# The norm of four mixers: squares summed into columns instead of rows, and the factor turned back into rows by a matmul

## Chip, cores, metric

The kernel runs on one core of a Trainium2 chip. The metric is the time of one execution in microseconds (us). The engines are TensorE (PE, with its weight loads PEld), VectorE (DVE), ScalarE (ACT), GpSimd (POOL) and the DMA queues of SyncE (SP). A program that is compiled from the kernel fixes the order of the instructions on each engine.

## What is computed

A network of two blocks over 256 tokens of width 1024, all in float32. The first block (attention, gated delta rule, mixture of experts) is not touched. The second has four layers, each a mixer and an MLP, each between norms:

```python
def rms_norm_2(x, gain):
    xf = x.astype(jnp.float32)
    y = xf * lax.rsqrt(jnp.mean(xf * xf, axis=-1, keepdims=True) + RMS_EPS) * gain.astype(jnp.float32)
    return y.astype(x.dtype)

def second_block(x, norm_gains, ...):
    h = x
    for i in range(DEPTH_2):                      # 4
        kind, j = i % N_MIXERS, i // N_MIXERS     # 3 kinds
        xn = rms_norm_2(h, norm_gains[i, 0])
        if kind == 0:
            m = stick_breaking_mixer(xn, sb_w_qkv[j], sb_w_o[j])
        elif kind == 1:
            m = short_conv_mixer(xn, conv_w_in[j], conv_w[j], conv_w_out[j])
        else:
            m = gla_mixer(xn, gla_w_in[j], ...)
        h = h + rms_norm_2(m, norm_gains[i, 1])
        f = squared_relu_mlp(rms_norm_2(h, norm_gains[i, 2]), ffn_w_up[i], ffn_w_down[i])
        h = h + rms_norm_2(f, norm_gains[i, 3])
    return h
```

The change concerns `rms_norm_2(h, norm_gains[i, 0])`, the norm ahead of each mixer. So the mixers come in the order stick-breaking, conv, GLA, stick-breaking.

## The kernel before

The residual is kept transposed: `hT` is 128 partitions x 8 chunks x 256 tokens, so the width lies across partitions and chunks and the tokens lie along the free axis. A norm therefore has to sum squares over partitions, which PE does.

Stages follow each other through `post` (L426). It turns the result of the stage before into `hT`, chunk by chunk (transposes L444, addition on DVE L447), and at once makes the operand of the next stage: `operand` splits gain x `hT` in two parts of reduced precision, `xh` (ACT, L348) and `xl` (DVE, L349). The matmuls of the mixer begin on these *un-normalised* operands. What is missing is one factor per token. It is applied when products leave PSUM: `ev_q` and `ev_k` (L723, L728) in the stick-breaking mixer, L582 in the conv mixer, L810 and L824 in GLA.

The factor `r` has the row form: 128 x 256, every partition the same. `pre` returns a function `factor()` that makes it when it is first asked for. For a mixer it does so in two steps, with a priority of 50 ahead of its place in the program:
- `sumsq(..., direct=8)`: eight squares on ACT (L324) and eight f32 matmuls `ones` x square, 128 x 256, into one PSUM bank of tag `s` (L337). With `ones` as the weights every partition gets the sums.
- `factor`: Ln (L290) and Exp (L291) on ACT, then four DVE instructions L294 to L297 for a corrected inverse root, all 128 x 256.

Where the mixer's values are evicted with tokens on the partitions, the factor is needed as a column per token. `columns` (L696) makes it from `r` with two transposes (L700) and a DVE copy. The two stick-breaking mixers and GLA do that.

Weights come by DMA as `raw` pieces of 128 x 1024, and `split` parts each into a cast `hi` (ACT, L190) and a rest `lo` (DVE, L193). The names `mg` and `split` are two further pairs of buffers for the same. `chunk` (L220) makes 128 columns of a product with 24 matmuls of 128 x 256: eight times `hi` x `xh` (L228) and `lo` x `xh` (L229), then eight of `hi` x `xl` (L231). `chunks` alternates the PSUM tags `g` and `s`; each tag has two banks. So a product that is not evicted holds its bank, and the third chunk of a tag waits for it.

The order on each engine is set by a scheduler at build time: it goes by priority, and `high_priority(offset)` moves a piece of the program ahead. Each engine then runs its instructions strictly in that order. The splits of the first weight pieces and the norm's root share DVE and ACT.

## Time and profile before

| | us |
|---|---|
| median of 3 runs | 1893.52 |
| lowest, highest | 1893.19, 1896.58 |
| profiled execution | 1894.69 |
| its span | 1892.9 |

The span is the time between the first and last recorded instruction; 1.8 us lie around it. PE is busy for 96% of it, DVE for 58%, ACT for 50%. The mean clock granted to PE is 0.988 of full speed. A row of a timeline has the start in us from the span's beginning, the duration, the engine, the line, the operation, its tiles as out<-in, the shape, and the number of records; in brackets stands how long the engine had been idle, and what ended that. A matmul of the sums leaves two records, so a pair of one-column sums is an x4. Consecutive matmuls overlap in the records, so the step from one start to the next tells what one costs.

### The profile page before, as it was taken

To read this page: it belongs to the slowest core of one execution; us is meant where nothing else is said; L and a number is where in the kernel's file an instruction comes from. 1 tells how busy PE (TensorE), PEld (TensorE's weight loads), DVE (VectorE), ACT (ScalarE), POOL (GpSimd) and SP (SyncE) were. 2 spreads that over 40 slices of the span, in tenths; PEclk is the share of its full clock that TensorE was granted. 3 is DMA by queue.
4 is the path that set the end of the run, shared out by engine and by line. 5 is a ranking of instruction groups with operands and counts; after the bars stand their busy time and mean duration, and the time that the engine had idled before them with its cause. 6 is when DMAs were issued, how large, how long until landed. Compare 5 with 4: busy or idle time off the path is not lost.

```text
span 1892.9 us, 31009 instructions
## 1 busy us (share of the span) xinstructions
PE 1825.3 (96%) x12535; PEld 1572.1 (83%) x12535; DVE 1097.2 (58%) x1964; ACT 951.5 (50%) x1743; POOL 105.2 (6%) x116
## 2 busy tenths in 40 slices
PE   6899998998999999999999999999999999999998
PEld 3787788866666798899999899979989988989996
DVE  4848547532332664765577665567775556547554
ACT  4536456322222575644454654465664447746443
POOL 2212112100000000000011000001000000000000
PEclk9899999999999999999999999999999999999999
DMA  9544386688999443555545555543446554345561
GB/s 328 178 164 144 96 275 255 217 309 329 408 396 392 132 148 124 167 183 195 180 154 185 171 180 198 182 143 113 134 156 196 183 191 131 131 138 184 176 197 45
DMA packets 196872, 369.46 MB, mean 195 GB/s; under 512 B 9204, under 2 KB 153012, under 8 KB 185204
## 3 DMA queue, kind: packets, MB, share of 16 engines
q1 hardware_dynamic: 193248, 362.77, 55.8%
q10 hardware_dynamic: 2900, 3.29, 0.5%
q8 instruction: 100, 1.64, 0.3%
q0 software_dynamic: 576, 1.37, 0.3%
q14 instruction: 48, 0.39, 0.1%
HBM read 364.77 MB, written 2.63 MB: 194 GB/s over the span
## 4 chain that ended last, share of the span: by engine, by line
PE 70%; ACT 4%; DVE 2%; issue 1%; POOL 0%; DVEq 0%; ACTq 0%; POOLq 0%
PE big L530 22%; PE g L228 8%; PE g L229 8%; PE g L231 7%; PE g L1808 4%; PE s L1848 3%; PE s L231 2%; PE s L228 2%; PE s L229 2%; PE s L337 1%; ACT sq L415 1%; ACT sbs L750 1%; ACT sbs L749 1%; PE big L1860 1%; PE s L1777 1%
## 5 line engine op out<-in xcount | busy, mean ns | idle before, releaser
L193 DVE TENSOR_TENSOR lo<-raw,hi 128x1024 fp32r<-128x1024 f32 x310 | 382.1, 1235 | 268.2 <-ACT hi L190 260.7
L190 ACT CAST hi<-raw 128x1024 fp32r<-128x1024 f32 x318 | 331.4, 1045 | 213.0 <-PE big L530 121.6
L228 PE MATMUL g<-xh,hi 128*128 128x256 f32 x1088 | 277.4, 290 | 8.8 <-DVE glal L810 3.6
L229 PE MATMUL g<-xh,lo 128*128 128x256 f32 x1088 | 272.9, 286 | 0.7 <-DVE lo L193 0.7
L228 PEld LDWEIGHTS g<-xh,hi 128*128 128x128 f32 x1088 | 208.5, 192 | 21.4 <-issue 6.0
L229 PEld LDWEIGHTS g<-xh,lo 128*128 128x128 f32 x1088 | 208.7, 192 | 3.4 <-DVE lo L193 0.9
L231 PE MATMUL g<-xl,hi 128*128 128x256 f32 x1088 | 155.0, 284 | 0.0
L231 PEld LDWEIGHTS g<-xl,hi 128*128 128x128 f32 x1088 | 141.0, 192 | 0.3 <-issue 0.2
L530 PE MATMUL big<-hi,yh 128*128 128x512 f32 x416 | 133.7, 392 | 0.0
L530 PE MATMUL big<-hi,yl 128*128 128x512 f32 x416 | 133.2, 390 | 0.0
L530 PE MATMUL big<-lo,yh 128*128 128x512 f32 x416 | 133.0, 390 | 0.0
L493 ACT ACTIVATE sq<-g 128x256 f32<-128x256 f32 x116 | 44.5, 384 | 166.9 <-PE g L231 166.6
L193 DVE TENSOR_TENSOR split<-raw,split 128x1024 fp32r<-128x1024 f32 x64 | 78.3, 1224 | 58.2 <-ACT split L190 58.1
L193 DVE TENSOR_TENSOR mg<-raw,mg 128x1024 fp32r<-128x1024 f32 x64 | 78.3, 1224 | 53.9 <-ACT mg L190 53.8
L190 ACT CAST split<-raw 128x1024 fp32r<-128x1024 f32 x64 | 66.9, 1045 | 62.7 <-PE big L530 40.5
L190 ACT CAST mg<-raw 128x1024 fp32r<-128x1024 f32 x64 | 66.9, 1046 | 50.2 <-PE big L530 32.6
L530 PEld LDWEIGHTS big<-lo,yh 128*128 128x128 f32 x416 | 78.1, 188 | 16.9
L530 PEld LDWEIGHTS big<-hi,yl 128*128 128x128 f32 x416 | 78.1, 188 | 16.6
L228 PE MATMUL s<-xh,hi 128*128 128x256 f32 x320 | 84.5, 296 | 3.6 <-DVE fv L294 2.5
L530 PEld LDWEIGHTS big<-hi,yh 128*128 128x128 f32 x416 | 75.4, 188 | 13.9 <-issue 0.3
L229 PE MATMUL s<-xh,lo 128*128 128x256 f32 x320 | 83.1, 292 | 2.2 <-DVE lo L193 2.2
L271 DVE TENSOR_TENSOR yl<-s,yh 128x256 fp32r<-128x256 f32 x76 | 32.1, 423 | 87.7 <-ACT yh L270 81.2
(575 smaller groups left out, 4090.6 us busy)
## 6 DMA issues: line engine op xcount, KB each, us to landing
raw<-in_ffn_w_up_dram SPq DMA_DIRECT2D x64, 1024.0 KB, 5.7
raw<-in_ffn_w_down_dram SPq DMA_DIRECT2D x64, 1024.0 KB, 4.8
raw<-in_w_mod_dram SPq DMA_DIRECT2D x24, 1024.0 KB, 6.7
raw<-in_sb_w_qkv_dram SPq DMA_DIRECT2D x24, 1024.0 KB, 5.2
raw<-in_w_in_dram SPq DMA_DIRECT2D x22, 1024.0 KB, 6.7
raw<-in_conv_w_in_dram SPq DMA_DIRECT2D x12, 1024.0 KB, 5.4
raw<-in_gla_w_in_dram SPq DMA_DIRECT2D x12, 1024.0 KB, 5.4
extra<-in_w_e_gate_dram SPq DMA_DIRECT2D x11, 1024.0 KB, 9.0
```

Source lines behind the costliest of these rows:

```text
L190: i = nc.scalar.copy(hi, piece)
L193: j = on.tensor_tensor(out=lo, in0=piece, in1=hi.bitcast(F32), op=ALU.subtract)
L228: mm(ps, hi[:, k, sl], xh[k], start=k == 0, stop=False)
L229: mm(ps, lo[:, k, sl], xh[k], start=False, stop=False)
L231: mm(ps, hi[:, k, sl], xl[k], start=False, stop=k == kn - 1)
L271: self.nc.vector.tensor_tensor(out=lo, in0=src, in1=hi.bitcast(F32), op=ALU.subtract)
L337: mm(ps, self.ones, t, start=i == 0, stop=i == len(terms) - 1)
L415: nc.scalar.activation(out=junk, in_=acc[t][half], func=AF.Square, accum_out=o)
L493: nc.scalar.activation(out=t, in_=ps, func=AF.Relu)
L530: mm(acc[t][half], x[:, t * P:(t + 1) * P], v[:, 0, half * 512:(half + 1) * 512], start=g + c + i == 0, stop=g + c == n - 1 and i == 2, sk ...
L1808: on(mm(gu[i][64 * j:64 * j + 64, :], xg[:, k, o0 + j * cap:o0 + (j + 1) * cap], W[j][k], start=k == 0, stop=k == KD - 1, skip_group_check ...
L1848: on(mm(yps[64 * j:64 * j + 64, :], aT[:, f * P + 64 * j:f * P + 64 * j + 64], W[j][f][:, half * 512:half * 512 + 512], start=f == 0, stop ...
```

## The change

The norm of the mixers is made by other instructions.
- The sums: `column_sums` takes the square as the *weights* and one column of ones as the moving operand: for each of eight chunks and each half of the tokens one f32 matmul of 128 x 1 (L412 of the changed kernel). The result is two columns with tokens on the partitions. A whole bank of tag `s` is taken for it.
- The root: `column_factor` does Ln, Exp and the four DVE instructions on 128 x 2 (L421 to L426).
- The row form: for each half of the tokens DVE multiplies `ones` by the factor column (`fq`, `fv`, L379), a matmul with the identity turns that into 128 rows of the factor (L380, in f32, into the other half of the same bank), and ACT copies both halves to `r` (L381).
- The columns are kept as `self.rcol` for the values, and `columns` with its transposes goes.
- From the root on, the priority is 2000 ahead instead of 50.

```diff
                     with self.tc.high_priority(offset=50):
-                        ps = self.sumsq([self.hT[:, k] for k in range(KD)], nc.gpsimd, direct=8)
-                        self.factor(ps, D, r)
+                        bank = self.gps("s")
+                        self.column_sums(bank[:, 0:2])
+                    with self.tc.high_priority(offset=2000):
+                        self.rcol = self.column_factor(bank[:, 0:2])
+                        for t in range(2):
+                            m = self.nt("fv", 1)[:, :P] if t else self.nt("fq", 1)[:, :P]
+                            nc.vector.tensor_scalar(out=m, in0=self.ones, scalar1=self.rcol[:, t:t + 1], scalar2=None, op0=ALU.mult)
+                            nc.tensor.matmul(bank[:, S + t * P:S + (t + 1) * P], m, self.c["ident"], start=True, stop=True)
+                        nc.scalar.copy(r, bank[:, S:])
...
+    def column_sums(self, ps):
+
+        nc, order = self.nc, []
+        for k in range(KD):
+            sq = self.nt("sq", 3)
+            nc.scalar.activation(out=sq, in_=self.hT[:, k], func=AF.Square)
+            for t in range(2):
+                order.append(nc.tensor.matmul(ps[:, t:t + 1], sq[:, t * P:(t + 1) * P], self.ones[:, 0:1], start=k + t == 0,
+                                              stop=k == KD - 1, skip_group_check=True))
+        self.after(order[1], order[0])
+
+    def column_factor(self, ps):
+
+        nc = self.nc
+        st = self.pn.tile([P, 8], F32, tag="rst", name="rst", bufs=2)
+        v, y, q, r = [st[:, i:i + 2] for i in range(0, 8, 2)]
+        nc.scalar.activation(out=y, in_=ps, func=AF.Ln, scale=1.0 / D, bias=self.eps[:, 0:1])
+        nc.scalar.activation(out=y, in_=y, func=AF.Exp, scale=-0.5)
+        nc.vector.tensor_scalar(out=v, in0=ps, scalar1=1.0 / D, scalar2=EPS, op0=ALU.mult, op1=ALU.add)
+        nc.vector.tensor_tensor(out=q, in0=y, in1=y, op=ALU.mult)
+        nc.vector.scalar_tensor_tensor(out=q, in0=q, scalar=-0.5, in1=v, op0=ALU.mult, op1=ALU.mult)
+        nc.vector.scalar_tensor_tensor(out=r, in0=q, scalar=1.5, in1=y, op0=ALU.add, op1=ALU.mult)
+        return r
...
-    def columns(self, rep, out):
-
-        ps = self.gps("s")
-        for t in range(2):
-            self.nc.tensor.transpose(ps[:, t * P:(t + 1) * P], rep[:, t * P:(t + 1) * P], self.c["ident"])
-        self.nc.vector.tensor_copy(out, ps[:, 0:S].rearrange("p (t q) -> p t q", q=P)[:, :, 0])
-
...
-        rc = self.tmp(2, tag="sbrc", bufs=1)
-        self.columns(r(), rc)
+        r()
+        rc = self.rcol
...
-        rc = self.tmp(2, tag="glrc", bufs=1)
-        self.columns(r(), rc)
+        r()
+        rc = self.rcol
```

The order of instructions changes with it. On PE in the conv mixer, the end of the sums; before, L337 is a row sum and L228, L229 and L231 are the matmuls of chunks (`hi` of tag `g` the first, of `s` the second):

```order
L229 MATMUL s<-xh,lo 128x256
L228 MATMUL s<-xh,hi 128x256
L337 MATMUL s<-sq,ones 128x256
L228 MATMUL g<-xh,hi 128x256
L229 MATMUL g<-xh,lo 128x256
L231 MATMUL g<-xl,hi 128x256 x8
```

and now, where L412 is a pair of column sums:

```order
L228 MATMUL g<-xh,mg 128x256
L228 MATMUL g<-xh,hi 128x256
L229 MATMUL g<-xh,lo 128x256
L231 MATMUL g<-xl,hi 128x256
L412 MATMUL s<-ones,sq 128x1 x2
L231 MATMUL g<-xl,hi 128x256 x2
L412 MATMUL s<-ones,sq 128x1 x2
L231 MATMUL g<-xl,hi 128x256 x5
```

The last sum has moved from ahead of the last `xh` matmuls of the first chunk to among its `xl` matmuls, and parts of the second and third chunk (`mg`) come before it: 44 matmuls of chunks stand ahead of the end of the sums. In GLA there are 33, in the first mixer 22, in the last 44.

On PE in the conv mixer, the passage from the third chunk to the fourth, whose weights are in `split`, before:

```order
L228 MATMUL g<-xh,mg 128x256
L229 MATMUL g<-xh,mg 128x256
L231 MATMUL g<-xl,mg 128x256 x8
L228 MATMUL s<-xh,split 128x256
L229 MATMUL s<-xh,split 128x256
```

and now:

```order
L229 MATMUL g<-xh,mg 128x256
L231 MATMUL g<-xl,mg 128x256 x8
L380 MATMUL s<-ident,fq 128x128
L380 MATMUL s<-ident,fv 128x128
L228 MATMUL s<-xh,split 128x256
L229 MATMUL s<-xh,split 128x256
```

The two products of the row form stand between the chunks, and the fourth chunk takes a bank of tag `s` behind them. In the first mixer they stand inside the third chunk, 37 matmuls behind the last sum and 13 ahead of the fourth chunk; in the last mixer behind the first, second and fourth chunk and four mask products (L739 before), ahead of the third.

On DVE in GLA, the splits (L193) and the root, before:

```order
L193 TENSOR_TENSOR lo<-raw,hi 128x1024
L294 TENSOR_SCALAR fv<-s 128x256
L193 TENSOR_TENSOR lo<-raw,hi 128x1024
L295 TENSOR_TENSOR fq<-fy 128x256
L193 TENSOR_TENSOR lo<-raw,hi 128x1024
L296 SCALAR_TENSOR_TENSOR fq<-fq,fv 128x256
L193 TENSOR_TENSOR mg<-raw,mg 128x1024
L297 SCALAR_TENSOR_TENSOR r<-fq,fy 128x256
L810 TENSOR_TENSOR glal<-g,r 128x256
```

and now:

```order
L193 TENSOR_TENSOR lo<-raw,hi 128x1024
L423 TENSOR_SCALAR rst<-s 128x2
L424 TENSOR_TENSOR rst<-rst 128x2
L193 TENSOR_TENSOR lo<-raw,hi 128x1024
L425 SCALAR_TENSOR_TENSOR rst<-rst 128x2
L193 TENSOR_TENSOR lo<-raw,hi 128x1024
L426 SCALAR_TENSOR_TENSOR rst<-rst 128x2
L193 TENSOR_TENSOR mg<-raw,mg 128x1024
L379 TENSOR_SCALAR fq<-ones,rst 128x128
L379 TENSOR_SCALAR fv<-ones,rst 128x128
L834 TENSOR_TENSOR glal<-g,r 128x256
```

One split fewer stands between the first and the second step of the root; three still stand between the second step and the builds. ACT has, in all four mixers, a cast, Ln, a cast, Exp, two or more casts and then the copy of `r`; before, it had the same without the copy. The order of DMA issues on SP is unchanged.

## Rows read from the trace of the kernel before

**Rows 1.** Page, busy time of an engine, and the chain that ended last by engine.
```profile
PE 1825.3 (96%) x12535; PEld 1572.1 (83%) x12535; DVE 1097.2 (58%) x1964; ACT 951.5 (50%) x1743; POOL 105.2 (6%) x116
...
PE 70%; ACT 4%; DVE 2%; issue 1%; POOL 0%; DVEq 0%; ACTq 0%; POOLq 0%
```
**Rows 2.** Windows: stretch, its length, busy PE PEld DVE ACT POOL, clock, DMA.
```profile
973.00:1040.00 67.00, 67.00 (x524) 65.35 (x523) 48.12 (x77) 28.40 (x32) 11.68 (x13) 1.00 0.57 183
...
1571.50:1588.00 16.50, 16.50 (x124) 15.46 (x122) 14.31 (x28) 11.99 (x23) 0.00 (x0) 1.00 0.39 127
```
**Rows 3.** Timeline of the conv mixer's norm: PE, ACT and DVE.
```profile
957.83 0.39 PE L228 MATMUL g<-xh,hi 128*128 128x256 f32 x1
...
964.38 0.47 ACT L290 ACTIVATE fy<-s,eps 128x256 f32<-128x256 f32 x1
...
964.75 1.04 ACT L190 CAST hi<-raw 128x1024 fp32r<-128x1024 f32 x1
...
965.69 0.41 ACT L291 ACTIVATE fy<-fy 128x256 f32<-128x256 f32 x1
...
965.98 1.21 DVE L193 TENSOR_TENSOR lo<-raw,hi 128x1024 fp32r<-128x1024 f32 x1
...
967.12 0.42 DVE L295 TENSOR_TENSOR fq<-fy 128x256 f32<-128x256 f32 x1
...
970.06 0.41 DVE L297 SCALAR_TENSOR_TENSOR r<-fq,fy 128x256 f32<-128x256 f32 x1
970.12 0.28 PE L228 MATMUL s<-xh,split 128*128 128x256 f32 x1
```
**Rows 4.** Timeline of GLA's norm, PE: its first matmul, and the wait.
```profile
1242.35 0.39 PE L228 MATMUL g<-xh,hi 128*128 128x256 f32 x1
...
1255.52 0.55 PE L228 MATMUL g<-xh,hi 128*128 128x256 f32 x1 [3.59 <-DVE glal L810]
```
**Rows 5.** Timeline of PE: a pair of one-column sums in an ffn.
```profile
829.35 0.50 PE L403 MATMUL g<-ones,ss 128*128 128x1 f32 x4
...
829.91 0.28 PE L229 MATMUL g<-xh,lo 128*128 128x256 f32 x1
830.03 0.29 PE L228 MATMUL g<-xh,hi 128*128 128x256 f32 x1
```
**Rows 6.** Timeline of PE: a row sum in GLA's norm.
```profile
1247.87 0.59 PE L337 MATMUL s<-sq,ones 128*128 128x256 f32 x2
...
1248.42 0.28 PE L229 MATMUL g<-xh,lo 128*128 128x256 f32 x1
```
**Rows 7.** Timeline of ACT and DVE: small instructions of another root.
```profile
951.65 0.20 ACT L420 ACTIVATE st<-st 128x1 f32<-128x1 f32 x1 [0.29 <-DVE st L419]
...
952.12 0.16 DVE L422 TENSOR_TENSOR st<-st 128x1 f32<-128x1 f32 x1 [0.50 <-ACT st L421]
```
**Rows 8.** Timeline of PE in the first block: two f32 products of 128 columns.
```profile
80.63 0.74 PE L1148 MATMUL big<-cst,dgm 128*128 128x128 f32 x4
81.21 0.51 PE L1149 MATMUL big<-dgg,cst 128*128 128x1 f32 x4
```
**Rows 9.** Timeline of PE in the last mixer: first chunk, mask products behind the fourth.
```profile
1571.54 0.39 PE L228 MATMUL s<-xh,hi 128*128 128x256 f32 x1
...
1586.73 0.50 PE L739 MATMUL big<-maskb,identb 128*128 128x384 bf16 x2
```
**Rows 10.** Timeline of PE in the first mixer: first chunk, fourth chunk.
```profile
643.36 0.39 PE L228 MATMUL g<-xh,hi 128*128 128x256 f32 x1 [1.53 <-ACT xh L348]
...
656.51 0.28 PE L228 MATMUL s<-xh,split 128*128 128x256 f32 x1
```
**Rows 11.** Timeline of PE in the first mixer: two transposes of r.
```profile
712.29 0.44 PE L700 MATMUL s<-ident,r 128*128 128x128 f32 x2
...
712.69 0.28 PE L691 MATMUL g<-lo,xh 128*128 128x256 f32 x1
```
**Rows 12.** Windows: a stretch behind GLA's wait.
```profile
1258.00:1261.00 3.00, 3.00 (x10) 1.97 (x10) 0.69 (x1) 2.15 (x4) 0.00 (x0) 0.50 0.02 6
```

## The prediction

> **What bounds the kernel now.** I read the page first: TensorE (PE) is busy for 96% of the span, and the chain that ended last runs through it for 70%, with 4% on ACT and 2% on DVE [rows 1]. The reader is to see that a matmul saved or added is worth its own time, and that work on DVE and ACT counts only where PE waits for it. So I looked second at the stretches in which the changed norm lies, one for each mixer of the second block. In the last mixer's PE is busy for the whole 16.50 us, and after the conv norm it stays busy for 67.00 of 67.00 us [rows 2]. There is no slack that could take a delay back. Third I read the timeline of each norm, row by row, to see which value PE gets last.
>
> In the conv norm PE begins its first chunk at 957.83, Ln starts on ACT at 964.38, the factor r is written by DVE at 970.06 + 0.41 = 970.47, and PE passes from the third chunk to the fourth at 970.12 without a pause [rows 3]. That is the point: before, no matmul needs r. It is applied when products are evicted, so PE runs on through sums, root and splits. Of the four mixers only GLA holds PE up for the factor, 3.59 us, since the gate product needs an evicted operand [rows 4].
>
> **The sums: a wash.** Removed are eight sums per mixer, `ones` x squares, 256 columns wide. Added are eight pairs with the squares as weights and one column. In the GLA norm a row sum starts at 1247.87 and one chunk matmul lies between it and the matmul that starts at 1248.42; a chunk matmul takes 0.12 (829.91 to 830.03 [rows 5]), so a row sum takes 1248.42 - 0.12 - 1247.87 = 0.43 [rows 6]. The trace has products with one column too: a pair of the ffn's token sums starts at 829.35, and after one chunk matmul the next stands at 829.91, so a pair takes 0.44 [rows 5]. It is the same operation in the same place (f32, two instructions, four records), so I take 8 x 0.44 against 8 x 0.43: +0.1 per mixer, counted at nothing. Should the row be mostly something else, the pair is worth less; a lower end of 0.1 makes a rival.
>
> The Trainium skill speaks against my price here: "TensorE: Matmul & The Clock Gate", section "Back-to-back issue gap", gives about 60 cycles for the fewest columns, which at 2.4 GHz would make four records 0.1 us, and the sums 2.8 us per mixer cheaper. The pair in the trace, 0.44, doesn't agree; the same page's section "LDWEIGHTS (loading the stationary operand)" has a load cost its columns / 1.2, some 107 ns for 128, four of which come near the row.
>
> **The root: columns in place of rows, but the same queue.** Four DVE instructions and two on ACT of 256 columns become small ones; added are two builds of ones x factor (DVE, 128x128), two f32 products with the identity (PE) and a copy of r on ACT. A small DVE instruction takes 0.16 [rows 7] against 0.41 [rows 3], a small ACT one 0.20 [rows 7] against 0.47 and 0.41 [rows 3]. A build lies between 0.16 and 0.41, I take 0.28; the copy of 256 columns I take as 0.45, by Ln's 0.47. DVE: 4 x 0.19 + 2 x 0.3 = 1.4 against at most 4 x 0.41 = 1.6: nothing. ACT: 0.2 + 0.2 + 0.45 against 0.47 + 0.41: nothing. What grows is the chain, since it is longer and PE is in it now.
>
> From the end T of the last column sum: Ln at T + 0.1 for 0.2; ACT's queue has a weight cast behind it, and casts step by 965.69 - 964.75 = 0.94 [rows 3]; then Exp 0.2, so that the first DVE product of the root can run at T + 1.5. The order in front.md shows three splits still standing between that and the build of `fq`, as before: a split and a small instruction step by 1.14 + 0.2 (965.98 to 967.12 [rows 3]). So 1.5 + 0.2 + 2 x 1.34 + 1.15 = 5.5: `fq` is built from T + 5.5. The name of the change says that the root comes ahead of the splits; in the order it doesn't. Builds end at T + 5.8 and T + 6.1, the two products at T + 6.6: two f32 products of 128 columns take 81.21 - 80.63 = 0.58 [rows 8], I count 0.55 with waits between. Copy on ACT 0.45: r at T + 7.05. PE's next chunk in a bank of tag `s` stands behind the products in PE's own order and needs the bank that the copy frees, so it starts at T + 7.1. Here PE waits twice where it waited for nothing: for the builds, and for the copy. Queued behind are all matmuls of the mixer.
>
> **T, mixer by mixer.** The order also moves the last column sums behind more chunk matmuls, since the scheduler pulls other chunks forward.
> - Conv: 44 chunk matmuls and eight pairs: T = 957.83 + 44 x 0.12 + 8 x 0.45 + 0.2 (first start) = 966.9, where the row sums were done before 964.38. Chunk four starts at 966.9 + 7.1 = 974.0 against 970.12 [rows 3]: +3.9.
> - GLA: 33 matmuls: T = 1242.35 + 4.0 + 3.6 + 0.2 = 1250.1. r at 1257.15, 0.3 later still if the clock is at half, then the gate eviction of 0.42; PE starts at 1258.0 against 1255.52 [rows 4]: +2.5.
> - Last mixer (stick-breaking): 44 matmuls: T = 1571.54 + 5.3 + 3.6 + 0.2 = 1580.6. Here the scheduler puts the fourth chunk ahead of the third, which then starts at 1587.7 and ends 24 x 0.12 = 2.9 later at 1590.6. Before, all four chunks and the first mask products were through at 1586.73 + 0.8 = 1587.5 [rows 9]: +3.1.
> - First mixer (stick-breaking): 22 matmuls: T = 643.36 + 2.6 + 3.6 + 0.2 = 649.8. Here the products stand inside the third chunk, 37 matmuls (4.4) behind T, and wait there until T + 5.85. They end at 656.4; 13 more matmuls, 1.6, and the fourth chunk starts at 658.0 against 656.51 [rows 10], the copy long done: +1.5, and up to 0.5 more if the squares come late; I take 1.7.
>
> **Removed behind that.** Three times the two transposes of r and a DVE copy. A pair starts at 712.29 and, after one chunk matmul, 712.69 follows: 0.28 [rows 11]; three of them 0.75, hidden by nothing. The DVE copy lies beside PE's work, nothing.
>
> Sum: 3.9 + 2.5 + 3.1 + 1.7 - 0.75 = **+10.45 us**. The profiled execution takes 1894.69 (span 1892.9 and 1.8 around it), 1.2 above the median of the three runs, 1893.52; the sum on the median gives **1904.0** (profiled: 1905.1). T can be off by 0.5 per mixer and the chain by 0.4, all the same way: 1900.5 to 1907.5.
>
> **Rivals.**
> - *The clock falls in the new pauses.* In GLA, PE's wait of 3.59 [rows 4] is followed by a stretch at a granted clock of 0.50, the level of 1.2 GHz [rows 12]. The records at that level run from 1255.5 to about 1261, 5.5 us at half rate: 2.75 lost. The new pauses of the conv mixer (3.3 in two pieces) and of the last mixer (2.2) are shorter than 3.59, but near it. For: the size. Against: the products fall into the pause. One fall gives 1906.8, two 1909.5.
> - *Part of the delay comes back.* If the last sums are nearer to the front than I count (pairs that overlap with the chunk beside them), or if the first mixer's products find their operands ready, two of the four delays shrink to 1 or less: +3 to +7, 1896 to 1900.5. Against: PE is busy in all of [rows 2].
> - *Columns are nearly free.* At 0.1 a pair, T comes 2.8 earlier in each mixer and PE has 2.8 less to do. Then conv +1.1 (971.2 against 970.12, PE waits for the same chain), GLA -0.3, last +0.3, first -0.8, transposes -0.75: -0.45, so 1893, no change. This is what the issue gap of the Trainium skill's "TensorE: Matmul & The Clock Gate" would bring; 0.44 in [rows 5] speaks against it.
> - *Faster.* It decides whether r is there when PE comes to the fourth chunk. If pairs are cheap and the splits between turn out to be done by then, nothing waits: 4 x (2.8 - 0.55) + 0.75 = 9.7 saved, 1884. For: fewer columns for PE. Against: the order has the splits there, each 1.21 on DVE [rows 3].
>
> **How the numbers follow.** Forecast 0.54, clock 0.20, part given back 0.13, free columns 0.08, faster 0.05. The range takes in the first three: 1896 to 1911; the likeliest alone is 1900.5 to 1907.5. A measurement of this kernel tells about 0.2% (3.8 us) from no change: under 1889.7 lies the fast case, 0.05; between there and 1897.3 lie the free columns and the low end of the part given back, 0.13; above, 0.82.
>
> **What would show it.** In the trace of the changed kernel: pairs of 0.44; the conv's Ln at about 967.0 in place of 964.4; `fq` built 5.5 after the last sum, with splits before it; waits of PE for `fq` of about 2.5 and for the copy of r of about 0.65 in the conv mixer, 1.6 and 0.65 in the last, 1.4 in the first; GLA's wait up from 3.6 to about 6; two transposes gone in three mixers. I am wrong if a pair takes much less than 0.4, if the build follows the last sum by under 4 us, or if the granted clock falls after the new pauses.

## The result, and the profile after

The changed kernel takes 1905.54 us, the median of 5 runs (1904.06 to 1911.12), beside 1893.52 for the kernel before on the same chip (5 runs, 1892.9 to 1896.58). The ratio is 1.0065 (95% interval 1.0052 to 1.0077): 12 us slower. The forecast was 1904.0, slower.

The share of busy time tells nothing of it: PE is busy for 96% of the span in both. What answers to [rows 4] is the list of PE's waits; the columns are the waiting instruction, what released it, us in total, times, and the longest:

```profile
PE s L380 <- DVE fq L379: 6.5, 3, 3.4
...
PE s L228 <- ACT r L381: 0.9, 2, 0.5
PE g L228 <- DVE glal L834: 0.9, 1, 0.9
```

All three lines are new, in this form: PE waits three times for the builds of the row form, twice for the copy of r, and in GLA for the gate eviction, where the one wait of 3.59 stood before. The conv mixer answers to [rows 3] (timeline: start, duration, engine, line, instruction, and in brackets the idle time and what ended it):

```profile
959.91 0.39 PE L228 MATMUL g<-xh,hi 128*128 128x256 f32 x1
...
967.74 0.50 PE L412 MATMUL s<-ones,sq 128*128 128x1 f32 x4
968.11 0.48 PE L231 MATMUL g<-xl,hi 128*128 128x256 f32 x2
968.43 0.50 PE L412 MATMUL s<-ones,sq 128*128 128x1 f32 x4
...
968.97 0.26 ACT L421 ACTIVATE rst<-s,eps 128x2 f32<-128x2 f32 x1 [1.94 <-PE s L412]
...
970.30 0.17 DVE L424 TENSOR_TENSOR rst<-rst 128x2 f32<-128x2 f32 x1 [0.88 <-ACT rst L422]
970.38 1.22 DVE L193 TENSOR_TENSOR lo<-raw,hi 128x1024 fp32r<-128x1024 f32 x1
...
971.58 1.22 DVE L193 TENSOR_TENSOR lo<-raw,hi 128x1024 fp32r<-128x1024 f32 x1
...
972.79 1.22 DVE L193 TENSOR_TENSOR lo<-raw,hi 128x1024 fp32r<-128x1024 f32 x1
973.93 0.28 DVE L379 TENSOR_SCALAR fq<-ones,rst 128x128 f32<-128x128 f32 x1
...
974.26 0.49 PE L380 MATMUL s<-ident,fq 128*128 128x128 f32 x2 [1.87 <-DVE fq L379]
...
975.01 0.37 ACT L381 COPY r<-s 128x256 f32<-128x256 f32 x1 [1.54 <-PE s L380]
975.43 0.58 PE L228 MATMUL s<-xh,split 128*128 128x256 f32 x1 [0.46 <-ACT r L381]
```

Read it downwards. A pair of column sums costs 968.43 - 967.74 - 2 x 0.12 = 0.45. Ln starts when the last is done; three splits of 1.22 stand between the second step of the root and the build; PE, idle, takes the products, and then waits for the copy. PE's first matmul of this mixer starts at 959.91, so the fourth chunk comes 15.52 behind it, against 970.12 - 957.83 = 12.29 before.

The same in GLA, with its first matmul, and in the last mixer:

```profile
1248.46 0.39 PE L228 MATMUL g<-xh,hi 128*128 128x256 f32 x1
...
1261.52 0.76 PE L380 MATMUL s<-ident,fq 128*128 128x128 f32 x2 [3.43 <-DVE fq L379]
...
1263.62 0.58 PE L228 MATMUL g<-xh,hi 128*128 128x256 f32 x1 [0.92 <-DVE glal L834]
```
```profile
1592.83 0.49 PE L380 MATMUL s<-ident,fq 128*128 128x128 f32 x2 [1.20 <-DVE fq L379]
...
1594.01 0.38 PE L228 MATMUL s<-xh,split 128*128 128x256 f32 x1 [0.46 <-ACT r L381]
```

In the first mixer PE has two waits that it didn't have before, of 0.44 each, one among the sums and one behind them for a cast, and none for the builds:

```profile
643.33 0.39 PE L228 MATMUL g<-xh,hi 128*128 128x256 f32 x1 [0.44 <-ACT xh L348]
...
656.88 0.39 PE L380 MATMUL s<-ident,fq 128*128 128x128 f32 x2
```

Four further stretches (windows: stretch, length, busy PE, PEld, DVE, ACT and POOL, granted clock, DMA share, GB/s), three windows in the first mixer and one in the conv mixer, and below them the first mixer's norm in the kernel before:

```profile
640.00:643.70 3.70, 3.14 (x23) 2.85 (x24) 3.70 (x9) 3.12 (x10) 0.87 (x1) 1.00 0.02 4
...
646.00:650.00 4.00, 4.00 (x20) 4.00 (x21) 1.23 (x1) 1.35 (x2) 0.00 (x0) 0.50 0.01 2
650.00:654.00 4.00, 3.56 (x15) 3.27 (x16) 2.37 (x5) 3.55 (x6) 0.00 (x0) 0.50 0.80 262
...
975.40:978.00 2.60, 2.57 (x12) 2.57 (x13) 1.56 (x5) 0.00 (x0) 0.83 (x1) 0.50 1.09 351
```
```profile
643.40:653.60 10.20, 10.20 (x64) 8.89 (x65) 8.82 (x17) 9.93 (x21) 0.70 (x1) 1.00 0.17 52
```

In the first mixer's norm the clock is at 1.00 in the window that ends just behind the wait among the sums, and at its lower level (0.50, 1.2 GHz) in the next two, while most of the column sums run; in 646.00:650.00 PE is busy throughout in the records. The kernel before was at 1.00 there. In the conv mixer the clock is at 0.50 behind the two new waits.

**Where the time went.** Stages are cut at the first chunk matmul of the first mixer and at the first transpose that ends each stage (L444 before, L475 after). The conv mixer so lasts 1060.60 - 957.00 = 103.60 after and 1054.16 - 954.92 = 99.24 before: +4.36.

```profile
957.00 0.38 PE L475 MATMUL big<-ident,pm 128*128 128x128 f32 x2
...
1060.60 0.38 PE L475 MATMUL big<-ident,pm 128*128 128x128 f32 x2
```
```profile
954.92 0.38 PE L444 MATMUL big<-ident,pm 128*128 128x128 f32 x2
...
1054.16 0.38 PE L444 MATMUL big<-ident,pm 128*128 128x128 f32 x2
```

Made in this way for every profile of this study, in us against the profile of before ("end" is the whole). Each row is one execution, which can lie several us from the median of its runs (e3's 4.4 below, e11's 5.2 above):

| profile | ahead | first | conv | GLA | last | four ffns | end |
|---|---|---|---|---|---|---|---|
| changed kernel | -3.24 | +5.64 | +4.36 | +1.21 | +2.80 | -1.42 | +9.35 |
| changed kernel, again (e8) | -0.27 | +7.16 | +4.64 | -0.05 | +2.81 | -1.38 | +12.91 |
| e1 rows, root first | +0.64 | +0.04 | +0.03 | -4.79 | 0.00 | +0.02 | -4.06 |
| e2 columns, root first | -1.91 | +5.04 | +0.45 | -1.68 | +0.88 | -1.39 | +1.39 |
| e3 columns, no products | -2.61 | +6.73 | +2.85 | +0.03 | +0.09 | -1.44 | +5.65 |
| e4 columns twice | -1.28 | +14.19 | +13.22 | +10.55 | +6.26 | -1.43 | +41.51 |
| e5 rows twice | -1.90 | +3.20 | +3.42 | -2.12 | +3.39 | -0.02 | +5.97 |
| e6 rows, idle columns | +0.90 | +2.90 | +3.50 | +3.43 | +3.48 | 0.00 | +14.19 |
| e7 rows in the first mixer | -0.26 | +2.19 | +4.39 | +1.10 | +2.80 | -1.43 | +8.79 |
| e9 columns, idle rows | -1.01 | +8.56 | +3.85 | +1.61 | +4.43 | -1.46 | +15.98 |
| e10 e1 with GLA's gate first | -0.41 | +0.03 | 0.00 | -5.75 | -0.02 | -0.02 | -6.15 |
| e11 filler in the pause | +2.71 | +6.98 | +4.65 | +1.32 | +2.80 | -1.41 | +17.05 |
| e12 rows, new chain | +0.06 | +0.86 | +0.92 | +0.32 | +0.90 | -1.44 | +1.62 |

What lies ahead of the first mixer is the first block, which none of these kernels touches; it differs by some 3 us to either side from execution to execution, much of it in stretches in which the clock is at the lower level. The mixers' columns repeat to within 0.3 where the kernels are alike there (conv 4.36, 4.64, 4.39, 4.65), apart from the first mixer and GLA, where a clock fall lies. The four ffns come out 0.3 to 0.45 shorter each in all kernels that have the new root in some mixer, e7's first ffn too, ahead of which the old root stands. In the first ffn of the changed kernel this builds up in small steps over the whole stage, without a wait that differs; its cause stays open.

### The profile page after: what moved, and what is told of

Same layout as the page of the kernel before. It is cut to its first block, busy times and chain, and to the rows that moved or that the text cites. A ratio compares the mean times of both kernels' runs of the same rounds, so it can differ in the third digit from the quotient of the medians.

```text
span 1902.2 us, 31148 instructions
## 1 busy us (share of the span) xinstructions
PE 1829.5 (96%) x12609; PEld 1577.9 (83%) x12609; DVE 1094.7 (58%) x1969; ACT 951.8 (50%) x1747; POOL 102.2 (5%) x116
## 4 chain that ended last, share of the span: by engine, by line
PE 70%; ACT 4%; DVE 2%; issue 1%; POOL 0%; DVEq 0%; ACTq 0%
PE big L561 22%; PE g L228 8%; PE g L229 7%; PE g L231 7%; PE g L1832 4%; PE s L1872 3%; PE s L228 2%; PE s L229 2%; PE s L231 2%; ACT sq L446 1%; ACT sbs L774 1%; ACT sbs L773 1%; PE big L475 1%; PE big L1884 1%; PE s L1801 1%
## 5 line engine op out<-in xcount | busy, mean ns | idle before, releaser
L193 DVE TENSOR_TENSOR lo<-raw,hi 128x1024 fp32r<-128x1024 f32 x310 | 382.0, 1235 | 271.7 <-ACT hi L190 269.5
L228 PE MATMUL g<-xh,hi 128*128 128x256 f32 x1088 | 278.5, 290 | 5.9 <-ACT dxp L1120 2.8
L229 PE MATMUL g<-xh,lo 128*128 128x256 f32 x1088 | 274.7, 287 | 0.7 <-DVE lo L193 0.7
L228 PEld LDWEIGHTS g<-xh,hi 128*128 128x128 f32 x1088 | 210.2, 193 | 17.9 <-ACT dxp L1120 4.2
L229 PEld LDWEIGHTS g<-xh,lo 128*128 128x128 f32 x1088 | 210.5, 193 | 3.5 <-DVE lo L193 0.9
L231 PE MATMUL g<-xl,hi 128*128 128x256 f32 x1088 | 158.0, 285 | 0.0
L231 PEld LDWEIGHTS g<-xl,hi 128*128 128x128 f32 x1088 | 142.5, 193 | 0.3 <-issue 0.2
L193 DVE TENSOR_TENSOR split<-raw,split 128x1024 fp32r<-128x1024 f32 x64 | 78.3, 1224 | 57.6 <-ACT split L190 57.5
L193 DVE TENSOR_TENSOR mg<-raw,mg 128x1024 fp32r<-128x1024 f32 x64 | 78.3, 1224 | 53.9 <-ACT mg L190 53.8
L228 PE MATMUL s<-xh,hi 128*128 128x256 f32 x320 | 83.5, 292 | 3.6 <-DVE fv L294 2.5
L229 PE MATMUL s<-xh,lo 128*128 128x256 f32 x320 | 82.9, 291 | 2.2 <-DVE lo L193 2.2
```

The source lines that it names most:

```text
L193: j = on.tensor_tensor(out=lo, in0=piece, in1=hi.bitcast(F32), op=ALU.subtract)
L228: mm(ps, hi[:, k, sl], xh[k], start=k == 0, stop=False)
L229: mm(ps, lo[:, k, sl], xh[k], start=False, stop=False)
L231: mm(ps, hi[:, k, sl], xl[k], start=False, stop=k == kn - 1)
```

## Experiments

**The theory** on record says that the chain from the last sum to r costs, since PE now stands in it, and that the splits between the root's steps make it long. **The rival** is that the one-column products themselves cost.

### e1: the kernel before, with the root ahead of the splits

```diff
-        nc.scalar.activation(out=y, in_=y, func=AF.Exp, scale=-0.5)
+        e = nc.scalar.activation(out=y, in_=y, func=AF.Exp, scale=-0.5)
...
-        nc.vector.scalar_tensor_tensor(out=out, in0=q, scalar=1.5, in1=y, op0=ALU.add, op1=ALU.mult)
+        return e, nc.vector.scalar_tensor_tensor(out=out, in0=q, scalar=1.5, in1=y, op0=ALU.add, op1=ALU.mult)
...
-                        self.factor(ps, D, r)
+                        self.hold = self.factor(ps, D, r)
```

`hold` is the pair of instructions behind which `split` orders its cast and its rest, from the fifth piece of a stage on.

> The kernel before, with its row sums and its 128x256 root, but every weight split from the fifth on is ordered behind the root: casts behind Exp, DVE rests behind the last step. Nothing of the column form is in it. Theory 'queue' (what costs is the chain from the last sum to r, and in it the splits between the steps of the root): r comes 2.7 us behind the last sum instead of 6, GLA's wait of 3.6 us and the 2.75 us of half clock behind it go, the other three mixers stay as they were since PE never waited there: 1887 (1885 to 1890). Rival 'columns' (what costs in the changed kernel are the one-column products themselves and the clock at them): this kernel has none, and its splits come later, so 1893.5 or a little above. Rival 'splits are needed early': 1895 to 1900, with PE waiting for a weight rest.

Measured: 1890.44 (7 runs, 1888.09 to 1891.3), just above the range; the kernel before took 1894.09 beside it, ratio 0.9975 (0.9963 to 0.9986). In the table all of it lies in GLA, -4.79; the other stages of the second block move by 0.04 at most. GLA's norm in the timeline:

```profile
1249.22 0.47 ACT L290 ACTIVATE fy<-s,eps 128x256 f32<-128x256 f32 x1 [0.52 <-PE s L337]
...
1251.10 0.42 DVE L297 SCALAR_TENSOR_TENSOR r<-fq,fy 128x256 f32<-128x256 f32 x1
...
1252.58 0.42 DVE L810 TENSOR_TENSOR glal<-g,r 128x256 f32<-128x256 f32 x1
...
1253.14 0.35 PE L228 MATMUL g<-xh,hi 128*128 128x256 f32 x1 [0.49 <-DVE glal L810]
```
```profile
1253.00:1256.00 3.00, 2.86 (x16) 2.21 (x17) 3.00 (x4) 1.12 (x2) 0.00 (x0) 1.00 0.68 208
```

r is done 2.3 behind the start of Ln, where in the trace of before r ended at 1254.91 and Ln began at 1248.82: 6.1.

```profile
1248.82 0.47 ACT L290 ACTIVATE fy<-s,eps 128x256 f32<-128x256 f32 x1
...
1254.50 0.41 DVE L297 SCALAR_TENSOR_TENSOR r<-fq,fy 128x256 f32<-128x256 f32 x1
```

The wait is 0.49 in place of 3.59, and the granted clock behind it (the window) stays at 1.00, where [rows 12] has 0.50. Theory 'queue' holds, with 3.7 of the 6.5 that it expected on the medians: 0.49 is the wait that is left, and a wait of 0.67 for `gla` (L818) later in GLA, which the kernel before didn't have, takes as much back. PE waits for no split here, so that splits are needed early is ruled out.

### e2: the changed kernel, with the root ahead of the splits

```diff
-        nc.scalar.activation(out=y, in_=y, func=AF.Exp, scale=-0.5)
+        self.root = nc.scalar.activation(out=y, in_=y, func=AF.Exp, scale=-0.5)
...
-                            nc.vector.tensor_scalar(out=m, in0=self.ones, scalar1=self.rcol[:, t:t + 1], scalar2=None, op0=ALU.mult)
+                            built = nc.vector.tensor_scalar(out=m, in0=self.ones, scalar1=self.rcol[:, t:t + 1], scalar2=None, op0=ALU.mult)
...
                         nc.scalar.copy(r, bank[:, S:])
+                    self.hold = (self.root, built)
```

> The changed kernel with the same order forced: splits from the fifth on behind Exp (casts) and behind the second build (rests). Column sums, row-form products and copy all stay. Theory 'queue': the builds come about 1.5 us behind the last sum instead of 5, PE waits some 0.4 for them and pays 0.55 for the products: +0.9 in each of three mixers, GLA about 1 earlier than before, transposes -0.75: 1894.5 (1892 to 1897). Rival 'columns': the sums are what they were, so 1902 or more.

Measured: 1897.07 (10 runs, 1895.27 to 1901.49), ratio 1.0015 (1.0005 to 1.0024). The conv norm, DVE and PE:

```profile
970.04 0.16 DVE L424 TENSOR_SCALAR rst<-s 128x2 f32<-128x2 f32 x1 [3.83 <-ACT rst L422]
...
970.86 0.29 DVE L379 TENSOR_SCALAR fq<-ones,rst 128x128 f32<-128x128 f32 x1
...
971.21 0.49 PE L380 MATMUL s<-ident,fq 128*128 128x128 f32 x2
```

The build follows 0.8 behind the root's first step on DVE, and PE doesn't wait for it. The sums stand where they stood: 44, 33 and 44 chunk matmuls come ahead of the last one in conv, GLA and the last mixer, as in the changed kernel. Conv falls from +4.36 to +0.45, GLA from +1.21 to -1.68, the last mixer from +2.80 to +0.88: 8.7 us in these three were the splits in the chain, with the clock fall in conv, which is gone too. What stays is the first mixer, +5.04, which this theory doesn't explain.

### e3: the changed kernel without products and copy

```diff
-                            m = self.nt("fv", 1)[:, :P] if t else self.nt("fq", 1)[:, :P]
+                            m = r[:, t * P:(t + 1) * P]
...
-                            nc.tensor.matmul(bank[:, S + t * P:S + (t + 1) * P], m, self.c["ident"], start=True, stop=True)
-                        nc.scalar.copy(r, bank[:, S:])
```

> The changed kernel without the two identity products and without the copy: DVE writes ones x factor column straight into r (so r holds the factor in the wrong orientation, and the mixers' results are not the reference's). Sums, root and splits between are kept. Theory 'queue': r is just as late as the builds are (about 5.8 behind the last sum), but PE no longer has to wait for it in its own order; what is left is the fourth of GLA's wait for the gate eviction (+1.2) and about 1 us in the conv and the last mixer where a bank waits for its eviction, less 0.75 for the transposes: 1895.5 (1893.5 to 1898). Rival 'columns': 1902 or more. Rival 'late r alone' (the evictions are what holds PE, the products are harmless): within 2 us of the changed kernel, 1903.5 to 1906.

Measured: 1904.66 (4 runs, 1900.29 to 1909.31), ratio 1.006 (1.0037 to 1.0083). My expectation missed. The median lies where the rival 'late r alone' put it, but the trace doesn't bear that out for all mixers. The last mixer does come back to +0.09 and GLA to +0.03, but conv keeps +2.85 and the first mixer has +6.73, with the clock at its lower level there. The conv mixer, where PE waits 2.82 for a bank:

```profile
975.66 0.48 DVE L379 TENSOR_SCALAR r<-ones,rst 128x128 f32<-128x128 f32 x2
976.05 1.22 DVE L193 TENSOR_TENSOR mg<-raw,mg 128x1024 fp32r<-128x1024 f32 x1
977.19 0.42 DVE L611 TENSOR_TENSOR cr<-r 128x256 f32<-128x256 f32 x1
978.04 1.23 DVE L193 TENSOR_TENSOR split<-raw,split 128x1024 fp32r<-128x1024 f32 x1 [0.43 <-ACT split L190]
979.18 0.42 DVE L619 TENSOR_TENSOR cc<-g,cr 128x256 f32<-128x256 f32 x1
...
979.75 0.36 PE L228 MATMUL g<-xh,hi 128*128 128x256 f32 x1 [2.82 <-DVE cc L619]
```

Two more splits stand between r and the first eviction, which I had not counted. So a late r, with two splits ahead of the evictions, holds PE in the conv mixer, by the two banks of a tag, even when no product waits for it.

### e4: every pair of column products twice

```diff
-            for t in range(2):
+            for t in range(4):
```

with the square's half taken by `t % 2`, four columns in place of two.

> The changed kernel with every pair of column products done twice (the second pair into two columns that nobody reads): 64 more one-column products. By the price of 0.44 to 0.45 a pair all of it lies on the path, since the waits follow the last sum at a fixed distance: 32 x 0.45 = +14.4 against the changed kernel, 1920 (1917 to 1923). If one-column products are nearly free (0.1 a pair): +3, 1908.5. If the clock falls at them, more than 1923.

Measured: 1935.28 (4 runs, 1929.96 to 1939.98), ratio 1.0211 (1.0183 to 1.024): 30 above the changed kernel, where the price of a pair makes 14.4. The rest is the clock (windows in the first mixer and in conv):

```profile
645.00:665.00 20.00, 20.00 (x95) 20.00 (x95) 8.48 (x17) 9.28 (x17) 0.00 (x0) 0.50 0.24 75
976.00:993.00 17.00, 17.00 (x82) 17.00 (x82) 4.44 (x8) 5.18 (x10) 0.00 (x0) 0.50 0.04 5
```

20 and 17 us at the lower level, with PE busy without a gap, and GLA's norm too, there with waits of PE. The last mixer's norm kept 1.00 and costs 6.26 - 2.80 = 3.5, eight pairs at 0.43. So the price per pair holds at the upper level, one-column products are not nearly free, and with twice as many of them the clock is low in three of the four norms; the fourth shows that the number alone doesn't decide it.

### e5 to e9: what brings the clock down in the first mixer?

e5 is the kernel before with each row sum done twice, e6 the kernel before with each row sum followed by the pair of column products, whose result nobody reads:

```diff
...
+            j = mm(bank[:, S:], self.ones, sq, start=False, stop=k == KD - 1, skip_group_check=True)
```
```diff
...
+            for t in range(2):
+                j = mm(bank[:, S + t:S + t + 1], sq[:, t * P:(t + 1) * P], self.ones[:, 0:1], start=False, stop=k == KD - 1,
+                       skip_group_check=True)
```

> The kernel before with every row sum of the four mixer norms done twice (the second into the other half of the bank, not read): 32 more matmuls of 256 columns, no one-column product. This and the next run ask why the granted clock fell at the first mixer's norm in all profiles with column sums so far, and in none with row sums. Theory 'form' (it is the one-column products): the clock stays up here, 32 x 0.43 = 13.8 on the path, a little less where GLA's wait hides it: 1906 (1904 to 1908). Rival 'later sums' (any sums that end later bring the fall, whatever their form): the sums end about as late here as in the changed kernel, so a fall of some 10 us at half rate in the first mixer: +4.5 more, 1911.

> The kernel before with its row sums and, beside each, the pair of one-column products of the changed kernel into columns that nobody reads; root and row form by the row sums as before. 32 pairs x 0.44 = 14.1 on the path. Theory 'form': the clock falls at the first mixer's norm too, some 10 us at half rate, 4.5 lost: 1912 (1910 to 1916), against 1906 for the run with doubled row sums. Rival 'later sums': the same as the run with doubled row sums, within 2 us. Rival 'the chain brings the fall' (products and waits behind the sums): no fall here, 1907.5.

Measured: e5 1901.67 (5 runs, 1899.96 to 1902.71), ratio 1.0036 (1.0022 to 1.0051), below its range for GLA's sake; e6 1908.14 (4 runs, 1907.72 to 1908.89), ratio 1.0073 (1.0056 to 1.009). In the table eight more row sums cost 3.2 to 3.4 in three mixers and eight pairs 2.9 to 3.5: the same price, as the prediction had it (GLA came out shorter by 2.12 in e5 in spite of them: in its order two splits stand ahead of the root on DVE and none between its steps, r is done 1.66 behind the start of the first step, and PE doesn't wait, so the chain theory speaks there again). Neither fell in the first mixer; e6, its norm:

```profile
648.00:653.00 5.00, 5.00 (x38) 4.79 (x39) 2.77 (x5) 3.75 (x8) 0.00 (x0) 1.00 0.11 21
```

So column products that have row sums beside them didn't bring the clock down.

e7 puts the norm of the first mixer alone back, e8 is the changed kernel again:

```diff
+                    self.norms = getattr(self, "norms", 0) + 1
+                if not ffn and self.norms == 1:
+                    with self.tc.high_priority(offset=50):
+                        ps = self.sumsq([self.hT[:, k] for k in range(KD)], nc.gpsimd, direct=8)
+                        self.factor(ps, D, r)
+                    self.rcol = self.tmp(2, tag="sbrc", bufs=1)
+                    self.columns(r, self.rcol)
+                elif not ffn:
...
```

> The changed kernel with the norm of the first mixer alone put back (row sums, 128x256 root, transposes for its column); conv, GLA and last mixer as changed. Theory 'form': the fall at the first mixer goes, and with it all of that mixer's +5.6: 1900 (1898 to 1901.5). Rival 'the fall is chance, or moves on to the next norm': 1903 to 1906. By the prediction's own term for that mixer (+1.7, less 0.28 for the transposes) it would be 1904.

> The changed kernel once more, for its profile and as the neighbour of the run above on the same chip: 1905.5 (1904 to 1907). Theory 'form': the clock falls at the first mixer's norm again. If it doesn't fall, the fall is chance: 1901 in that execution.

Measured: e7 1902.59 (4 runs, 1901.97 to 1903.42), ratio 1.0043 (1.0027 to 1.006); e8 1907.47 (4 runs, 1905.2 to 1908.35), ratio 1.0068 (1.0051 to 1.0085). The fall came again in e8, with +7.16 in the first mixer, and not in e7. But e7 keeps +2.19 there and misses its 1900: my edit asks for the transposes of r at once, and PE waits at them and at a split.

```profile
652.00 0.38 PE L229 MATMUL g<-xh,mg 128*128 128x256 f32 x1 [1.03 <-DVE mg L193]
...
655.28 0.44 PE L739 MATMUL s<-ident,r 128*128 128x128 f32 x2 [0.27 <-DVE r L297]
```

e9 is the changed kernel with idle row sums beside its column products:

```diff
...
+            order.append(nc.tensor.matmul(spare, self.ones, sq, start=False, stop=k == KD - 1, skip_group_check=True))
...
```

> The changed kernel, and beside each pair of column products the row sum of the kernel before (into the other half of the bank, not read; the products of the row form overwrite it). Root, products, copy and splits are as changed. The run with row sums and column pairs, but the old root, kept its clock at the first mixer, so it is open whether the fall there needs the missing row sums or the new chain behind the sums. Theory 'missing row sums': the granted clock stays at 1.00 at the first mixer's norm; the row sums cost 3.4 in three mixers and 2 in GLA, the waits for the builds shrink (37 chunk matmuls instead of 28 stand between): 1911 (1908 to 1913). Rival 'chain': the fall is there as in the changed kernel: 1915 or more.

Measured: 1908.11 (4 runs, 1905.58 to 1910.65), ratio 1.0062 (1.0046 to 1.0079). Here the fall came, with row sums between the pairs:

```profile
645.00:649.00 4.00, 4.00 (x16) 3.65 (x17) 2.03 (x5) 3.01 (x7) 0.00 (x0) 0.50 0.00 0
```

Theory 'missing row sums' falls in this form, though the time lies in the range that it gave: the row sums put 22 chunk matmuls ahead of the last sum in place of 44 in conv and the last mixer, PE no longer waits for the builds there, and that pays for part of what they cost.

### e11: filler in PE's pause ahead of the first mixer

```diff
-            self.warm(y, 3)
+            self.warm(y, 6)
```

> The changed kernel with three more filler matmuls (ones x a tile, the result not read; the kernel has three there already) in the 1.5 us pause of PE ahead of the first mixer; the mask products that stood ahead of the pause move in between the column sums. All six profiles with the column norm in the first mixer showed the granted clock fall there during the sums, none of the six with the old norm did, and neither the row sums nor the column pairs alone decide it. Theory 'pause': it is the pause of PE ahead of light sums; with it filled the clock stays at 1.00 in the first mixer, which then comes out near the prediction's +1.7 instead of +5.6 to +7.2: 1902 (1900 to 1903.5). Rival 'not the pause': the fall is there as before, 1905.5 to 1907.5.

Measured: 1906.55 (4 runs, 1904.42 to 1911.74), ratio 1.0066 (1.0049 to 1.0083). The pause shrank from 1.53 to 0.57 and the clock fell all the same (+6.98 in the first mixer). A pause of 1.53 isn't needed for the fall, nor does it bring one: the kernels without a fall have it too.

### e12: row sums with the new chain behind them

```diff
-                        self.column_sums(bank[:, 0:2])
+                        self.column_sums(bank[:, 0:S])
...
-            for t in range(2):
-                order.append(nc.tensor.matmul(ps[:, t:t + 1], sq[:, t * P:(t + 1) * P], self.ones[:, 0:1], start=k + t == 0,
-                                              stop=k == KD - 1, skip_group_check=True))
-        self.after(order[1], order[0])
+            nc.tensor.matmul(ps, self.ones, sq, start=k == 0, stop=k == KD - 1)
```

> The changed kernel with the sums of the kernel before (one row sum in place of each pair of column products); the root, the builds, the products and the copy are as changed, but the root reads the first two columns of the row sums, so the factor is not the reference's. No one-column product is left. The order puts the last sum behind 19 to 22 chunk matmuls in place of 33 to 44, and 51 chunk matmuls instead of 28 between it and the products in the conv mixer. Theory 'chain from the last sum': the builds are still 5 us behind the last sum, but 51 x 0.12 = 6.1 covers that, so no wait of PE; the products cost 0.55 in each of four mixers, the transposes save 0.75: conv +0.5, last +0.5, GLA about 0, 1894.5 (1892 to 1897). If the products alone cost (bank, copy): 1899 or more. On the clock at the first mixer's norm: if it falls there all the same (first mixer +5 and more, 1899), the new chain brings it; if not (first mixer +0.5), the one-column products in place of row sums do.

Measured: 1896.88 (10 runs, 1893.73 to 1900.36), ratio 1.0013 (1.0002 to 1.0023). Three mixers cost 0.86 to 0.92 each, GLA 0.32. In the conv mixer the build comes late as before, and PE has enough in front of the products:

```profile
970.27 0.28 DVE L379 TENSOR_SCALAR fq<-ones,rst 128x128 f32<-128x128 f32 x1
...
970.60 0.49 PE L380 MATMUL s<-ident,fq 128*128 128x128 f32 x2
```

No wait stands in brackets. (In GLA PE still waits 2.6 for the build and 0.9 for the gate eviction; before the change it waited 3.59.) The window of its first mixer:

```profile
646.00:650.00 4.00, 3.62 (x21) 3.10 (x20) 2.32 (x7) 3.93 (x10) 0.00 (x0) 1.00 0.00 0
```

So the root on columns, the builds, products and copy cost less than 1 us a mixer where the sums end early. The rest of the 12 us is what the column sums do: in conv, GLA and the last mixer the scheduler lets 33 to 44 chunk matmuls go ahead of the last of them in place of 19 to 22, so that too few are left to cover the chain, and the clock falls in the first mixer. With row sums this chain has its cover; with the root ahead of the splits (e2) it is short enough without it.

### e10: the version that beats both

```diff
-            nc.vector.tensor_tensor(out=al, in0=ps, in1=r(), op=ALU.mult)
+            i = nc.vector.tensor_tensor(out=al, in0=ps, in1=r(), op=ALU.mult)
             nc.vector.memset(al[0:1, :], 1.0)
+            self.hold = (self.hold[0], i)
```

on top of e1, in GLA.

> The kernel before with the root ahead of the splits, as in the first run, and in GLA also the eviction of the gate product ahead of them (in the first run one split of 1.2 us stood between r and that eviction, and PE waited 0.49 for it). By the 'queue' theory 0.5 less in GLA than in the first run, nothing elsewhere: 1890 (1888.5 to 1891). If the split that moves back makes a later chunk wait, as much comes back: 1890.5 to 1891.5.

Measured: 1887.88 (5 runs, 1887.24 to 1889.86), ratio to before 0.9961 (0.9947 to 0.9975), 0.6 below the range. GLA comes to -5.75, 0.96 less than in e1, where 0.5 was expected. The eviction of the gate follows r at once, and PE waits next for a split:

```profile
1250.55 0.43 DVE L810 TENSOR_TENSOR glal<-g,r 128x256 f32<-128x256 f32 x1
...
1252.16 0.39 PE L229 MATMUL g<-xh,lo 128*128 128x256 f32 x1 [0.47 <-DVE lo L193]
```

It takes the order from the change's idea (the root ahead of the splits) and leaves the columns.

## Why the prediction was right, point by point

- **Sums.** A pair was priced at 0.44 and costs 0.45 in the changed kernel; eight cost as much as eight row sums (e5, e6). A wash at the upper clock, as said. The rival of nearly free columns is out by the 0.45. The section "Back-to-back issue gap" of the Trainium skill's "TensorE: Matmul & The Clock Gate" would have brought it only by its table, which is for an isolated matmul: it says itself that the table's formula under-counts at few columns, where weight loads have no share in it. The trace bears the caveat out: 0.45 for the four records of a pair, against some 0.1 by the table.
- **Conv, +3.9.** Ln was to start 9.2 behind the first chunk matmul (967.0 against 957.83) and started 968.97 - 959.91 = 9.06 behind. The build was to follow Ln by 5.4 and followed by 4.96; the waits were 1.87 and 0.46 for 2.5 and 0.65. The fourth chunk came 15.52 - 12.29 = 3.2 late. The stage lost 4.36, since the clock fell at the waits: the rival's mechanism, at 1.1 in place of its price of 2.75. By the prediction's own list that fall was a sign of being wrong; it is met here, at a small cost.
- **GLA, +2.5.** The gate's matmul came at 1263.62, 15.16 behind the first, against 13.17 before: +2.0, of which the stage kept 1.21. Its waits rose to 3.43 + 0.92, where about 6 was said; the half clock behind the pause stayed.
- **Last, +3.1.** The stage lost 2.80, with waits of 1.20 and 0.46 for 1.6 and 0.65, and the clock didn't fall.
- **First, +1.7.** This is the term that was mis-sized: +5.64 and +7.16. The foreseen wait of 1.4 at the products is not there at all. Instead the clock fell while the sums ran, so the chunk ahead of the products took longer than the chain. The prediction reckoned with falls behind the new pauses only, not at the new sums. With row sums ahead of it, and no fall, the new chain costs this mixer 0.86 (e12).
- **Transposes, -0.75.** They are gone; their share can't be read apart from the stages. Three pairs at 0.28 are 0.84, not 0.75. (In the rival of free columns the first mixer's -0.8 should be 1.7 - 2.8 = -1.1. Nothing hangs on either.)
- **The sum.** The four mixers cost 14.0 in place of 10.45, the ffns gave back 1.4 that the prediction didn't have, and in the first profile the first block was 3.2 shorter by chance. On the medians the change costs 12.0 and, in the second comparison, 1907.47 - 1894.35 = 13.1. So the middle came out 1.5 to 2.7 low, for the fall in the first mixer; the forecast's own range (to 1907.5) held it. That it came so near is in part luck: the first mixer lay 3.9 and 5.5 above its term in the two profiles, and GLA (1.3 and 2.6 below) and the ffns, neither of which the sum had right, took more than half of that back.
- **The mechanism.** That the splits in the chain make the wait is shown by e2 (conv, GLA and the last mixer cost 8.4 in the changed kernel and -0.35 without them) and by e1 in the kernel before. What the prediction took as a given, the late place of the column sums, is as much a cause: e12 has the same splits in the chain and, with the sums ahead, no wait of any size but GLA's. It changes the form of the sums and their place together; no run has column sums at the early place, so that the place alone does it is argued from the equal price of the two forms.

## What to carry to other kernels

A priority is no order: ask the built program which bulk work stands between the steps of a short chain that someone waits for, and tie the bulk work behind the chain's last step. Before a step is moved onto the engine that bounds, count how much work that engine has between the chain's start and the step; the chain is free only as long as that covers it. Fewer columns in a matmul saved nothing here, since a one-column f32 product cost as much per square as the row form.

## What the runs showed of the hardware

Not expected: PE can be busy for the whole of a long stretch in the records and be granted the lower clock all the same (20.00 of 20.00 us busy at 0.50 in e4, the columns done twice). The kernels whose first mixer had the column sums and the new root showed a fall there in 7 of 7 profiles, those without both in 0 of 7. What starts it stays open: column pairs with row sums beside them and the old root kept 1.00 (e6), the same two with the new root did not (e9), row sums with the new root did (e12), and shrinking the pause ahead changed nothing (e11). Nor do short waits among the sums sort the profiles: the changed kernel's fall comes behind one of 0.44, but e12 has one of 0.38 in the same place and kept 1.00, and e4 and e9 have none and fell.
